# Modulation blocks computed two to a PSUM bank, and a new order for the opening stage of a two-layer trunk kernel

## Chip, cores, metric

The kernel runs on one core of one Trainium2 chip. The metric is the device time of one execution in microseconds (us); the time before is the median of three executions.

## What is computed

Two layers of a trunk are applied to 128 context tokens and 256 latent tokens of width 1024. Each layer is: a modulated RMSNorm and a SwiGLU feed-forward of width 2816, a modulated RMSNorm and a mixer (attention, a gated convolution of 31 taps, a long convolution with learned filters), and a second feed-forward. The parts that matter here:

```python
def trunk_layer(x, cond, l, P, cache):
    mod = (jax.nn.silu(cond) @ P['w_mod'][l] + P['b_mod'][l])[:, None, :]
    sh1, sc1, g1, sh2, sc2, g2, sh3, sc3, g3 = jnp.split(mod, N_MOD, axis=-1)
    h = rmsnorm(x, P['g_ffn1'][l]) * (1 + sc1) + sh1
    x = x + 0.5 * g1 * swiglu(h, P['w1_gate'][l], P['w1_up'][l], P['w1_down'][l])
...
def hyena_filters(L, w1, b1, f1, w2, b2, f2, w3, log_decay):
...
    h = jnp.sin(f1.astype(F32) * (z @ w1.astype(F32) + b1.astype(F32)))
    h = jnp.sin(f2.astype(F32) * (h @ w2.astype(F32) + b2.astype(F32)))
    h = (h @ w3.astype(F32)).reshape(L, HYENA_ORDER, 2, HYENA_W)
    decay = jnp.exp(log_decay.astype(F32)).reshape(HYENA_ORDER, 2, HYENA_W)
    h = h * jnp.exp(-tn[:, None, None, None] * decay[None])
```

The first feed-forward cannot start before the shift `sh1` and scale `sc1` of layer 0 exist for the slice of channels it contracts over. The filters depend on weights alone, and their spectra are needed much later, by the mixers.

## The kernel before

**Layout.** Activations lie with channels on the 128 partitions and the 384 tokens along the free axis: `x` is eight tiles of 128x384. Weights come as a stream of 512 KB chunks, each eight blocks of 128x128 (`raw`, five buffers). ScalarE casts a chunk to `hi` (L249), VectorE makes the remainder `lo` (L250), and each block is multiplied by three matmuls (`mm3`, L263 to L265): hi by hi, hi by lo, lo by hi.

**Opening.** `startup` (L1058) walks a list of letters, `STARTUP`, and issues what each stands for. A scheduler then places the instructions into the engines' queues; each engine runs its own queue strictly in the order given. The letters are: `z`, `c`, `e`, `w`, `f` load constants and filter weights; `M` with a number is one modulation block; `X` with a number loads one tile of `x`, makes its modulated form (`hidden`, L387, tile `h`) and its square; `G` is one step of the first matrix product, four column blocks times one `h`, 12 matmuls; `F` is the next piece of the filter generator; `R` and `S` are the norm; `D` with a number is a row of dummy matmuls on a matrix of ones (`spin`, L1053), as many as the tuple `SPIN` says, besides 12 at the start.

**A modulation block** (`mod_start`, L287) makes shift and scale of one of the eight channel tiles for both conditions. Two chunks of `w_mod` (tile `raw`, from `wms`) are multiplied by the 32-column matrix `scond`, of which two columns hold the conditions and 30 are zero, into four 32-row strips of a PSUM bank of tag `at` (L293). ScalarE copies the bank (L297), TensorE transposes it in two matmuls (L300), VectorE adds the strips up and finishes the numbers (L304, L310, L313). Every 32-bit matmul shows as two records in the profile.

**The filter generator** (`filters`, L946) yields after each piece. Two sine stages come first (L949 and L954 on TensorE, seven VectorE operations each, L938 on ScalarE). `filter_time` (L964) then makes three time groups per layer: ScalarE takes exponentials of the decay (L975, L976, tile `P`), TensorE makes two products that share the array by row halves (L979, PSUM tag `sp`, two banks), VectorE multiplies them (L984) and forms sums and differences (L990, tiles `hy` and `H`). `filter_freq` (L1013) makes three spectra per layer: two from those filters (L674), one from the 31 convolution taps, whose matmuls have 16 rows (L1032). Each spectrum goes through one buffer `sw` and is written to memory by a GpSimd-issued transfer (`Hd`, L1040), so a spectrum's buffer is free only when the previous one is written.

The rest (feed-forward, mixer, both layers) follows. Modulation of all later places is done on VectorE (L324) beside the matrix products.

Of the kernel before, what the change touches and what calls it, by code (L numbers as in the profile page):

```python
# [11 lines left out]
F32 = mybir.dt.float32  # L12
# [5 lines left out]
D, DEPTH, NP, NS, PAST = 1024, 2, 128, 256, 128  # L18
T = NP + NS
TB = T + 2  # L20
KT = D // 128
# [18 lines left out]
START_TILES = ["a0", "x11", "g0", "v0"]  # L40
PROGRAM = ("v1 x10 a1 H g1 H H q1 k q0 C v A C q3 q2 C A A H A H C A A x21 A V A A x20 C V A H C V C A V A W W W "
           "V V V W W W W W W W W W W W W W").split()
STARTUP = ("z c F F M4 D1 e M0 D2 w X0 M1 F M7 G M2 F X1 X2 M5 G M3 F X3 F F X4 F G M6 G X5 F G G F X6 X7 f G R F F S "
           "G F").split()
SPIN = (12, 3, 6)
LATE = {5: "cond", 12: "cst"}
MOD0 = {(0, 0): 5, (0, 2): 5, (1, 0): 5, (1, 2): 4}
RSTD = (3, 6)
# [144 lines left out]
class Kernel:  # L193
# [90 lines left out]

    def mod_start(self, kb):  # L287
        nc = self.nc
        ps = self.psum("at")[:, 0:256]
        for half in range(2):  # L290
            raw = self.raw(self.d["wms"][kb, half])
            for j in range(4):
                nc.tensor.matmul(ps[32 * j:32 * j + 32, :], lhsT=self.scond[:, half * 4 + j, :],  # L293
                                 rhs=raw[:, j * 256:(j + 1) * 256], start=half == 0, stop=half == 1,
                                 tile_position=(0, 32 * j))
        row = self.t(256)
        nc.scalar.copy(out=row, in_=ps)  # L297
        tp = self.psum("at")[:, 0:256]
        for b in range(2):
            nc.tensor.transpose(tp[:, b * 128:(b + 1) * 128], row[:, b * 128:(b + 1) * 128], self.ident)  # L300
        v = tp.rearrange("p (b j i) -> p b i j", b=2, j=4, i=32)[:, :, 0:2, :]
        for kind in range(2):
            m = self.mods[0, 0, kind][:, 2 * kb:2 * kb + 2]
            nc.vector.tensor_reduce(out=m, in_=v[:, 1 - kind], axis=AX.X, op=ALU.add)  # L304
            self.mod_finish(0, 0, kind, 2 * kb, 2)

    def mod_finish(self, l, sub, kind, o, n):
        nc = self.nc
# [704 lines left out]
    def filter_freq(self, l, G):  # L1013
        nc = self.nc
        cw = self.S("cv", (96, 768))
        nc.sync.dma_start(out=cw, in_=self.d["cw"][l])
        taps = self.S("P", (96, 512))
        for ri, op in enumerate((ALU.add, ALU.subtract)):
            ready = nc.vector.tensor_tensor(out=taps[:, ri * 256:ri * 256 + 256], in0=cw[:, 0:256], in1=cw[:, 256:512],
                                            op=op)  # L1020
        for o in range(3):
            H = self.S("sw", (128, 3, 512))
            if o < 2:
                src = [[G[o, t][:, ri * 256:(ri + 1) * 256] for ri in range(2)] for t in range(3)]
                U = self.dft(src[2], 2), self.dft(src[1], 1)
            else:
                U = self.psum("sp"), self.psum("sp"), self.psum("at")
                for ri in range(2):
                    for u, t in zip(U, (2, 1, 0)):
                        rows = slice(32 * t, 32 * t + 16)  # L1030
                        with self.tc.high_priority(offset=PAIR * (2 * ri + 2 - t > 0)):
                            mm = nc.tensor.matmul(u[:, ri * 256:ri * 256 + 256],  # L1032
                                                  lhsT=cw[rows, 512 + 128 * ri:640 + 128 * ri],
                                                  rhs=taps[rows, ri * 256:ri * 256 + 256], start=True, stop=True,
                                                  tile_position=(32 * t, 0))
                        if ri == 0 and t == 2:
                            self.after(mm, ready)
            self.butterfly(U[0], U[1], H[:, 2, :], H[:, 1, :])
            nc.scalar.copy(out=H[:, 0, :], in_=self.dft(src[0], 0) if o < 2 else U[2])
            nc.gpsimd.dma_start(out=self.Hd[l, o], in_=H)  # L1040
            yield
# [16 lines left out]
    def startup(self, cols, tags):  # L1058
        nc, cp = self.nc, self.cp
# [1 line left out]
        self.filt, self.decay, self.hs, box = self.filters(), {}, [], []  # L1061
        accs = [self.psum(t) for t in tags]
        self.idle = accs[3][:, 388:512]
        self.spin(SPIN[0])
        step = 0
        for n in STARTUP:
            k = int(n[1:] or 0)
# [12 lines left out]
            elif n == "c":  # L1080
                self.loaded.add("early")
                nc.sync.dma_start(out=self.csts[:, 128:EARLY], in_=self.d["cst"][:, 128:EARLY])
            elif n[0] == "D":
                self.spin(SPIN[k])
            elif n[0] == "M":
                self.mod_start(k)
            elif n[0] == "X":
# [16 lines left out]
    def run(self):  # L1104
        nc, cp = self.nc, self.cp
# [7 lines left out]
        nc.gpsimd.memset(self.ones, 1.0)  # L1113
        self.mhalf = cp.tile([128, 16], F32, name="mhalf")
        nc.gpsimd.memset(self.mhalf, -0.5)
        self.scond = cp.tile([128, KT, 32], F32, name="scond")
        nc.gpsimd.memset(self.scond, 0.0)
        nc.scalar.activation(out=self.scond[:, :, 0:2], in_=self.vec("cond", 0, 16).rearrange("p (k i) -> p k i", i=2),
                             func=AF.Silu)
        self.nsink = []  # L1120
        for l in range(DEPTH):
# [89 lines left out]
```

## Time and profile before

| | us |
|---|---|
| median of 3 executions | 1510.0 (1508.61 to 1513.52) |
| the profiled execution | 1510.81 |
| its span in the profile | 1509.0 |
| TensorE busy | 1482.5 (98% of the span) |
| VectorE busy | 1116.2 (74%) |
| ScalarE busy | 673.3 (45%) |
| first matmul of the first product step | at 27.52 |
| first matmul after the opening | at 72.70 |

Busy time is what the profile's records cover; a stretch in which TensorE reads as fully busy can still be slow when its granted clock is half. The granted clock is given as a share: 1.00 is 2.4 GHz, 0.50 is 1.2 GHz. "Idle before" in a row is how long the engine had stood still, with what ended the wait behind the arrow.

### The profile page before, as it was taken

To read this page: it belongs to the slowest core of one execution; us is meant where nothing else is said; L and a number is where in the kernel's file an instruction comes from. 1 tells how busy PE (TensorE), PEld (TensorE's weight loads), DVE (VectorE), ACT (ScalarE), POOL (GpSimd) and SP (SyncE) were. 2 spreads that over 40 slices of the span, in tenths; PEclk is the share of its full clock that TensorE was granted. 3 is DMA by queue.
4 is the path that set the end of the run, shared out by engine and by line. 5 is a ranking of instruction groups with operands and counts; after the bars stand their busy time and mean duration, and the time that the engine had idled before them with its cause. 6 is when DMAs were issued, how large, how long until landed. Compare 5 with 4: busy or idle time off the path is not lost.

```text
span 1509.0 us, 22131 instructions
## 1 busy us (share of the span) xinstructions
PE 1482.5 (98%) x8372; PEld 1401.0 (93%) x8372; DVE 1116.2 (74%) x2115; ACT 673.3 (45%) x1164; POOL 29.7 (2%) x72
## 2 busy tenths in 40 slices
PE   8999999999999999999999999999999999999997
PEld 4799999999968999999999999999996799999885
DVE  6799998776896789897558998755599577555342
ACT  6673333335476653224336333333547665333331
POOL 0100000000000000000000000000000000000000
PEclk9899999999999999999999999999999999999999
DMA  9847876565312357676444777644431135444531
GB/s 312 301 151 249 270 261 227 189 204 181 118 64 70 112 189 237 219 235 209 154 135 133 247 244 237 225 154 155 143 125 49 59 109 167 154 154 140 182 112 42
DMA packets 72651, 260.97 MB, mean 173 GB/s; under 512 B 8224, under 2 KB 9760, under 8 KB 72544
## 3 DMA queue, kind: packets, MB, share of 16 engines
q1 hardware_dynamic: 71360, 254.30, 51.4%
q0 software_dynamic: 1184, 5.25, 0.9%
q8 instruction: 66, 1.08, 0.3%
q14 instruction: 41, 0.34, 0.1%
HBM read 252.96 MB, written 6.56 MB: 172 GB/s over the span
## 4 chain that ended last, share of the span: by engine, by line
PE 92%; DVE 3%; ACT 3%; DMA 1%; issue 1%; SPq 0%; POOL 0%; POOLq 0%; DVEq 0%; ACTq 0%
PE acc L263 14%; PE acc L264 14%; PE acc L265 14%; PE S L265 12%; PE S L263 12%; PE S L264 12%; PE sp L474 2%; PE at L474 2%; PE sp L674 2%; PE acc L474 1%; PE S L474 1%; PE sp L720 1%; DVE lo L250 1%; DMA raw<-wmod 1%; DMA raw<-wms 0%
## 5 line engine op out<-in xcount | busy, mean ns | idle before, releaser
L250 DVE TENSOR_TENSOR lo<-raw,hi 128x1024 fp32r<-128x1024 f32 x313 | 381.7, 1222 | 209.1 <-ACT hi L249 160.2
L249 ACT CAST hi<-raw 128x1024 fp32r<-128x1024 f32 x313 | 327.0, 1049 | 390.7 <-issue 131.3
L324 DVE SCALAR_TENSOR_TENSOR junk<-raw,cb 128x1024 f32<-128x1024 f32 x256 | 312.7, 1221 | 49.8 <-DMA raw<-wmod 46.8
L263 PE MATMUL acc<-h,hi 128*128 128x384 f32 (+1 forms) x960 | 331.0, 345 | 0.0
L265 PE MATMUL acc<-h,lo 128*128 128x384 f32 (+1 forms) x960 | 326.0, 340 | 0.5 <-DVE lo L250 0.5
L264 PE MATMUL acc<-h,hi 128*128 128x384 f32 (+1 forms) x960 | 325.4, 340 | 0.6 <-DVE h L918 0.6
L263 PE MATMUL S<-h,hi 128*128 128x384 f32 (+1 forms) x768 | 259.9, 338 | 1.0 <-DVE x L435 1.0
L265 PE MATMUL S<-h,lo 128*128 128x384 f32 (+1 forms) x768 | 259.5, 338 | 0.0
L264 PE MATMUL S<-h,hi 128*128 128x384 f32 (+1 forms) x768 | 259.4, 338 | 0.0
L264 PEld LDWEIGHTS acc<-h,hi 128*128 128x128 f32 x960 | 181.0, 189 | 5.8 <-issue 3.1
L263 PEld LDWEIGHTS acc<-h,hi 128*128 128x128 f32 x960 | 180.5, 188 | 6.1 <-issue 3.9
L265 PEld LDWEIGHTS acc<-h,lo 128*128 128x128 f32 x960 | 181.5, 189 | 2.0 <-issue 0.8
L263 PEld LDWEIGHTS S<-h,hi 128*128 128x128 f32 x768 | 144.5, 188 | 2.0 <-issue 1.9
L265 PEld LDWEIGHTS S<-h,lo 128*128 128x128 f32 x768 | 145.0, 189 | 0.4 <-issue 0.3
L264 PEld LDWEIGHTS S<-h,hi 128*128 128x128 f32 x768 | 144.6, 188 | 0.4 <-issue 0.4
L393 ACT ACTIVATE h<-x,mod 128x128 fp32r<-128x128 f32 x96 | 41.5, 453 | 91.3 <-DVE x L435 89.4
L531 DVE TENSOR_TENSOR t<-S,t 128x384 f32<-128x384 f32 x72 | 39.8, 552 | 20.5 <-PE S L265 20.5
L281 ACT CAST P<-t 128x384 fp32r<-128x384 f32 x24 | 12.3, 514 | 71.4 <-DVE t L531 71.4
L530 ACT ACTIVATE t<-acc 128x384 f32<-128x384 f32 x72 | 34.8, 483 | 11.2 <-PE acc L265 11.2
L394 DVE SCALAR_TENSOR_TENSOR h<-x,mod,h 128x128 fp32r<-128x128 f32 x96 | 38.3, 415 | 1.2
L414 DVE TENSOR_TENSOR t<-acc,rb 128x384 f32<-128x384 f32 x44 | 24.3, 552 | 16.3 <-PE acc L265 16.3
L408 ACT ACTIVATE t<-t,mod,mod 128x128 f32<-128x128 f32 x64 | 31.7, 541 | 6.4 <-DVE t L405 6.4
(492 smaller groups left out, 2196.6 us busy)
## 6 DMA issues: line engine op xcount, KB each, us to landing
raw<-stream SPq DMA_DIRECT2D x313, 512.0 KB, 4.0
raw<-wmod SPq DMA_DIRECT2D x128, 512.0 KB, 4.3
raw<-wms SPq DMA_DIRECT2D x16, 512.0 KB, 6.6
Hd<-sw POOLq DMA_DIRECT2D x6, 768.0 KB, 4.6
H<-Hd SPq DMA_DIRECT2D x6, 768.0 KB, 4.9
x<-x SPq DMA_DIRECT2D x8, 192.0 KB, 6.2
y<-h SPq DMA_DIRECT2D x6, 256.0 KB, 2.1
cb<-crow SPq DMA_DIRECT2D x2, 512.0 KB, 5.3
```

Of the source, the lines that this page charges most:

```text
L249: nc.scalar.copy(out=hi, in_=raw)
L250: nc.vector.tensor_tensor(out=lo, in0=raw, in1=hi.bitcast(F32), op=ALU.subtract)
L263: nc.tensor.matmul(out, lhsT=w[0], rhs=x[0], start=start, stop=False)
L264: nc.tensor.matmul(out, lhsT=w[0], rhs=x[1], start=False, stop=False)
L265: nc.tensor.matmul(out, lhsT=w[1], rhs=x[0], start=False, stop=stop)
L324: nc.vector.scalar_tensor_tensor(out=self.junk, in0=raw, scalar=1.0, in1=self.cb[:, ci, :], op0=ALU.mult, op1=ALU.mult, accum_out=m[:, 2 * ...
L393: nc.scalar.mul(out=hl[:, 0, a:b], in_=self.x[k][:, a:b], mul=sc)
L394: nc.vector.scalar_tensor_tensor(out=hl[:, 1, a:b], in0=self.x[k][:, a:b], scalar=sc, in1=hl[:, 0, a:b].bitcast(F32), op0=ALU.mult, op1=AL ...
L408: nc.scalar.activation(out=t[:, a:b], in_=t[:, a:b], func=AF.Identity, scale=A[:, i:i + 1], bias=B[:, i:i + 1])
L474: nc.tensor.matmul(accs[b], lhsT=hid[2 * c + e][xi][:, b * 128:(b + 1) * 128], rhs=w[e][wi], start=c == 0 and left[b] == 5, stop=c == NFF ...
L530: nc.scalar.activation(out=s, in_=gp[:, :T], func=AF.Silu)
L531: nc.vector.tensor_tensor(out=s, in0=up[:, :T], in1=s, op=ALU.mult)
```

## The change

Three edits, all in the opening stage.

1. `mod_start` takes a pair of channel tiles. The matrix `scond` gets 34 columns, with the conditions in columns 2 and 3. The first tile of a pair multiplies by columns 2 to 33 and the second by columns 0 to 31, so their results fall on rows 0, 1 and rows 2, 3 of each strip and accumulate in one bank. One copy, one pair of transposes and one set of VectorE operations then serve two tiles. The 64 matmuls and the 16 chunks remain.
2. `STARTUP` is a new list: pairs in rising order, without the two rows of dummy matmuls, and with 10 dummies in place of 12 at the start.
3. The spectrum of the taps is made second of three instead of last.

```diff
-STARTUP = ("z c F F M4 D1 e M0 D2 w X0 M1 F M7 G M2 F X1 X2 M5 G M3 F X3 F F X4 F G M6 G X5 F G G F X6 X7 f G R F F S "
-           "G F").split()
-SPIN = (12, 3, 6)
+STARTUP = ("z c F F M0 e w X0 F X1 M1 F G F X2 G X3 F M2 F G X4 F G X5 M3 F X6 X7 G F G f F G R F F S G F").split()
+SPIN = 10
...
-    def mod_start(self, kb):
+    def mod_start(self, pair):
         nc = self.nc
         ps = self.psum("at")[:, 0:256]
-        for half in range(2):
-            raw = self.raw(self.d["wms"][kb, half])
-            for j in range(4):
-                nc.tensor.matmul(ps[32 * j:32 * j + 32, :], lhsT=self.scond[:, half * 4 + j, :],
-                                 rhs=raw[:, j * 256:(j + 1) * 256], start=half == 0, stop=half == 1,
-                                 tile_position=(0, 32 * j))
+        for e in range(2):
+            for half in range(2):
+                raw = self.raw(self.d["wms"][2 * pair + e, half])
+                for j in range(4):
+                    nc.tensor.matmul(ps[32 * j:32 * j + 32, :],
+                                     lhsT=self.scond[:, half * 4 + j, 2 - 2 * e:34 - 2 * e],
+                                     rhs=raw[:, j * 256:(j + 1) * 256], start=half + e == 0, stop=half + e == 2,
+                                     tile_position=(0, 32 * j))
...
-        v = tp.rearrange("p (b j i) -> p b i j", b=2, j=4, i=32)[:, :, 0:2, :]
+        v = tp.rearrange("p (b j i) -> p b i j", b=2, j=4, i=32)[:, :, 0:4, :]
         for kind in range(2):
-            m = self.mods[0, 0, kind][:, 2 * kb:2 * kb + 2]
+            m = self.mods[0, 0, kind][:, 4 * pair:4 * pair + 4]
             nc.vector.tensor_reduce(out=m, in_=v[:, 1 - kind], axis=AX.X, op=ALU.add)
-            self.mod_finish(0, 0, kind, 2 * kb, 2)
+            self.mod_finish(0, 0, kind, 4 * pair, 4)
...
-        for o in range(3):
+        for o in (0, 2, 1):
```

The lines of `mod_start` and above shift by one against the kernel before (L293 stays the line of the modulation matmuls; the copy is L298, the transposes L301, the exponentials L976 and L977, the half-array products L980, the tap matmuls L1033, the cast L248).

**ScalarE, from its first sine to the cast of the first weight chunk.** In the rows `cv` is the output of the second sine, `pt` the decay, `P` the exponentials, `sqs` and `t` after L343 and later squares of `x`, `h` the modulated `x`. Before:

```order
L938 ACTIVATE t_128<-t_131 128x384
L975 ACT_TABLE_LOAD
L975 ACTIVATE pt_181<-pt_181 128x512
L297 COPY t_168<-at_155 128x256
L976 ACTIVATE P_253<-pt_181,csts 128x512
L975 ACTIVATE pt_183<-pt_183 128x512
L938 ACT_TABLE_LOAD
L938 ACTIVATE cv_141<-t_144 64x384 x4
L297 COPY t_198<-at_185 128x256
L343 ACTIVATE sqs_226<-x 128x384
L976 ACT_TABLE_LOAD
L976 ACTIVATE P_254<-pt_183,csts 128x512
```

Now:

```order
L939 ACTIVATE t_126<-t_129 128x384
L939 ACTIVATE cv_139<-t_142 64x384 x4
L298 COPY t_178<-at_153 128x256
L976 ACT_TABLE_LOAD
L976 ACTIVATE pt_188<-pt_188 128x512
L344 ACTIVATE sqs_204<-x 128x384
L977 ACTIVATE P_208<-pt_188,csts 128x512
L394 ACTIVATE h_197<-x,mod_86 128x128
L394 ACTIVATE h_197<-x,mod_86 128x256
L976 ACTIVATE pt_190<-pt_190 128x512
L394 ACTIVATE h_224<-x,mod_86 128x128
L977 ACTIVATE P_209<-pt_190,csts 128x512
```

The two sines follow each other with no table load between them, and the two `pt` exponentials and the first `P` stand behind the second sine instead of ahead of it. Behind these rows, and still ahead of the cast of the first chunk (`hi_276`), now come the rest of `h_224`, one square, and the remaining four `P`.

**TensorE, up to the third half-array product.** `S` of L1055 is the dummy row, `at` a modulation bank, `sp` the products. Before:

```order
L293 MATMUL at_155<-raw_162,scond 32x256 x3
L300 MATMUL at_170<-csts,t_168 128x128 x2
L1055 MATMUL S_108<-ones 128x124 x3
L293 MATMUL at_185<-raw_186,scond 32x256 x4
L293 MATMUL at_185<-raw_192,scond 32x256 x4
L979 MATMUL sp_251<-kv_214,cv_141 128x512
L979 MATMUL sp_252<-kv_214,cv_141 128x512
L300 MATMUL at_200<-csts,t_198 128x128 x2
L1055 MATMUL S_108<-ones 128x124 x6
L293 MATMUL at_228<-raw_229,scond 32x256 x4
```

Now:

```order
L293 MATMUL at_153<-raw_172,scond 32x256 x4
L980 MATMUL sp_206<-kv_192,cv_139 128x512
L980 MATMUL sp_207<-kv_192,cv_139 128x512
L301 MATMUL at_180<-csts,t_178 128x128 x2
L293 MATMUL at_234<-raw_235,scond 32x256 x4
L293 MATMUL at_234<-raw_241,scond 32x256 x4
L980 MATMUL sp_292<-kv_192,cv_139 128x512
```

The dummies between the blocks are gone, and so is one pair of transposes.

**TensorE, at the tap matmuls of layer 0.** `acc` is the first product, `sqs` the sum of squares. Before:

```order
L362 MATMUL sp_664<-ones,sqs_226 128x1 x3
L1032 MATMUL sp_677<-P_557,cv_555 128x256 x2
L1032 MATMUL sp_678<-P_557,cv_555 128x256 x2
L263 MATMUL acc_105<-h_632,hi_648 128x386
L979 MATMUL sp_691<-kv_215,cv_141 128x512
L264 MATMUL acc_105<-h_632,hi_648 128x386
```

Now:

```order
L293 MATMUL at_462<-raw_481,scond 32x256 x4
L301 MATMUL at_489<-csts,t_487 128x128 x2
L1033 MATMUL at_563<-P_502,cv_500 128x256 x2
L1033 MATMUL sp_561<-P_502,cv_500 128x256
L1033 MATMUL sp_562<-P_502,cv_500 128x256
...
L980 MATMUL at_674<-kv_193,cv_139 128x512
L262 MATMUL acc_105<-h_414,hi_544 128x386
```

The cut leaves out the second matmul into each of `sp_561` and `sp_562`. All six tap matmuls now stand together, directly behind the last modulation pair and ahead of the fifth product step; before, two of them stood inside the fourth of the eight steps, and four ahead of the eighth.

## Rows read from the trace of the kernel before

**Rows 1.** The page: busy us, share of the span, instructions of each engine.

```profile
PE 1482.5 (98%) x8372; PEld 1401.0 (93%) x8372; DVE 1116.2 (74%) x2115; ACT 673.3 (45%) x1164; POOL 29.7 (2%) x72
```

**Rows 2.** Stretches of 10 us: busy us (instructions) per engine, granted clock, transfer share, GB/s.

```profile
10.00:20.00 10.00, 7.97 (x45) 3.57 (x46) 5.28 (x19) 8.46 (x14) 0.00 (x0) 0.83 1.03 399
20.00:30.00 10.00, 7.75 (x64) 4.33 (x63) 9.02 (x33) 9.37 (x17) 0.00 (x0) 1.00 0.84 285
...
60.00:70.00 10.00, 10.00 (x23) 5.09 (x19) 7.08 (x14) 5.14 (x9) 1.00 (x2) 0.56 0.71 252
```

**Rows 3.** What TensorE waited for, first 130 us: total us, times, longest.

```profile
PE at L293 <- DMA raw<-wms: 2.3, 2, 1.7
PE acc L265 <- DVE lo L250: 0.5, 1, 0.5
```

**Rows 4.** ScalarE in order of time: start us, us, line, operation, idle before.

```profile
11.05 1.28 ACT L975 ACT_TABLE_LOAD   x1
12.34 0.63 ACT L975 ACTIVATE pt<-pt 128x512 f32<-128x512 f32 x1
15.35 1.28 ACT L938 ACT_TABLE_LOAD   x1
16.64 2.15 ACT L938 ACTIVATE cv<-t 64x384 f32<-64x384 f32 x4
...
21.67 0.79 ACT L393 ACTIVATE h<-x,mod 128x128 fp32r<-128x128 f32 x2
...
24.89 1.32 ACT L976 ACTIVATE P<-pt,csts 128x512 f32<-128x512 f32 x2
26.12 0.35 ACT L297 COPY t<-at 128x256 f32<-128x256 f32 x1
26.37 1.04 ACT L249 CAST hi<-raw 128x1024 fp32r<-128x1024 f32 x1
...
31.95 0.94 ACT L346 ACTIVATE t<-x 128x384 f32<-128x384 f32 x2
```

**Rows 5.** VectorE in order of time, same columns.

```profile
15.69 0.36 DVE L936 TENSOR_SCALAR t<-t 128x384 f32<-128x384 f32 x1
...
27.86 1.22 DVE L250 TENSOR_TENSOR lo<-raw,hi 128x1024 fp32r<-128x1024 f32 x1
...
34.15 0.42 DVE L990 SCALAR_TENSOR_TENSOR hy<-P 128x256 f32<-128x256 f32 x1
```

**Rows 6.** TensorE in order of time, same columns.

```profile
14.24 0.44 PE L300 MATMUL at<-csts,t 128*128 128x128 f32 x2 [0.49 <-ACT t L297]
14.52 0.83 PE L1055 MATMUL S<-ones 128*128 128x124 f32 x6
15.28 1.07 PE L293 MATMUL at<-raw,scond 128*32 128x256 f32 x16
...
27.52 0.42 PE L263 MATMUL acc<-h,hi 128*128 128x386 f32 x1
...
59.16 1.45 PE L1032 MATMUL sp<-P,cv 16*128 16x256 f32 x8
...
63.56 0.53 PE L263 MATMUL S<-h,hi 128*128 128x386 f32 x1
63.88 0.53 PE L264 MATMUL S<-h,hi 128*128 128x386 f32 x1
...
72.70 0.44 PE L263 MATMUL acc<-h,hi 128*128 128x386 f32 x1
...
77.06 0.34 PE L263 MATMUL S<-h,hi 128*128 128x386 f32 x1
```

**Rows 7.** Stretches of 1 us on TensorE: busy us, granted clock, transfer share, GB/s.

```profile
61.00:62.00 1.00, 1.00 (x2) 0.60 0.71 172
...
71.00:72.00 1.00, 1.00 (x6) 0.78 0.91 324
```

**Rows 8.** The page's transfer issues: operation, count, KB each, us from issue to landing.

```profile
Hd<-sw POOLq DMA_DIRECT2D x6, 768.0 KB, 4.6
```

More of the change, by code (lines that the diff above doesn't have):

```diff
@@ L1063, in startup @@
         self.idle = accs[3][:, 388:512]
-        self.spin(SPIN[0])
+        self.spin(SPIN)
         step = 0
@@ L1082, in startup @@
                 nc.sync.dma_start(out=self.csts[:, 128:EARLY], in_=self.d["cst"][:, 128:EARLY])
-            elif n[0] == "D":
-                self.spin(SPIN[k])
             elif n[0] == "M":
@@ L1115, in run @@
         nc.gpsimd.memset(self.mhalf, -0.5)
-        self.scond = cp.tile([128, KT, 32], F32, name="scond")
+        self.scond = cp.tile([128, KT, 34], F32, name="scond")
         nc.gpsimd.memset(self.scond, 0.0)
-        nc.scalar.activation(out=self.scond[:, :, 0:2], in_=self.vec("cond", 0, 16).rearrange("p (k i) -> p k i", i=2),
+        nc.scalar.activation(out=self.scond[:, :, 2:4], in_=self.vec("cond", 0, 16).rearrange("p (k i) -> p k i", i=2),
                              func=AF.Silu)
```

## The prediction

> **What bounds the kernel now.** I read the page first: TensorE is busy for 1482.5 of 1509.0 us, VectorE for 74% [rows 1]. From 27.52 us on, TensorE reads as full almost to the end, so the sum of its work sets the end there, and a gain can come only from three things: an earlier start of that full stretch, less TensorE work in it, or a better clock. The new queues differ from the old only in the first 200 us or so; behind that they hold the same instructions in the same order. So I compare one mark: the first matmul behind the opening, at 72.70 us [rows 6]. What shifts it shifts the end.
>
> Second, the stretches of 10 us. Between 10 and 30 us TensorE is busy 7.8 to 8.0 us in ten, some of it with dummies, while ScalarE is busy 8.5 and 9.4 [rows 2]. The transfers run near full, yet TensorE waited for a modulation chunk only 2.3 us in all [rows 3]. So ScalarE's queue, not the arrival of bytes, sets when the first product step starts: its row that ends at 27.41 us is the cast of the first weight chunk, and the first product matmul follows at 27.52 [rows 4, 6].
>
> Third, the clock. Between 60 and 70 us the granted clock is 0.56 [rows 2]; it falls soon after 61 us and is back soon after 71 [rows 7]. The fall comes after the tap matmuls of 16 rows at 59.16. At 1.2 GHz product matmuls start 0.32 us apart (63.56 to 63.88); at 2.4 GHz, 24 of them take 77.06 - 72.70 = 4.36 us, 0.18 each [rows 6]. Ten us at half clock cost about 5.0 us.
>
> **The change, part by part.** The sum is made against the profiled execution, 1510.81 us with a span of 1509.0; it stands 0.8 above the median of 1510.0.
>
> 1. *Second sine.* Its table load ran from 15.35 to 16.63, and the last VectorE operation it depends on ended at 16.05 [rows 4, 5]. Without the reload, and with two fewer dummies ahead of the first sine (0.83/6 = 0.14 us for each record, four records, covered in part by the arrival of its input), the sine starts at about 15.85: **0.8 us earlier**. The rest of that load was waiting time anyway. The Trainium skill, "ScalarE: Activation LUTs", section "What ACT_TABLE_LOAD costs", puts a switch at about 2.66 us, a drain of 1.38 after the load included. The rows show the next activation 1.29 us after the load starts (11.05 to 12.34) and no drain, so the trace differs; by the page's figure the start of the product would come about 1.4 us earlier than I say.
>
> 2. *ScalarE from the second sine to the first cast.* The queue now holds behind the sine what was done in its shadow before: two `pt` exponentials (0.63 each) and one more `P` (0.66, half of 1.32). Two instructions for the second tile's `h` (0.7 of path, from 0.79) and one square (0.47, half of 0.94) also go ahead of the cast. One copy less returns 0.35 [rows 4]. That is 1.26 + 0.66 + 0.7 + 0.47 - 0.35 = **2.7 us later**. Together with step 1, the first product step starts at 27.52 - 0.8 + 2.7 = 29.4; I take 29.5.
>
> 3. *TensorE work from there to the mark.* It took 72.70 - 27.52 = 45.2 us. Off come 5.0 for the half clock, 0.5 for a wait on the first `lo` [rows 3], and 0.6 for the two pairs of transposes saved behind this point (at most 0.44 each [rows 6]). This leaves **39.1 us**. The modulation matmuls are as many as before, and at the first step half of them are done in both versions.
>
> 4. *Waits that the new order opens.* Behind the first two steps and the third pair's matmuls (29.5 + 24 x 0.18 + 2 x 1.07 = 36.0) stands the transform of the third time group. Its `hy` came 5.5 us after the end of the first `lo` (29.08 to 34.57 [rows 5]). `lo` now ends at about 30.7, and another tile's `h` (0.8) stands ahead, less 0.3 for small operations saved: ready at 36.7, a wait of 0.7. The last pair's transposes now stand directly behind its matmuls, so the copy is bare: 0.5, as at 14.24 [rows 6]. The fifth step's cast stands behind two squares and four `h` instructions that wait for those transposes: 0.94 + 1.6 + 1.04 of ScalarE and about 1.4 on VectorE, against 2.1 of tap matmuls and 0.9 of a lone half-array product; 0.8 is bare. A spectrum of the seventh step needs a bank that ScalarE empties only behind three casts and five exponentials: I put 1.1. Sum **3.1 us**; if VectorE and ScalarE run ahead it is 0, if each is half as long again 4.6.
>
> 5. *Dummies.* The nine in the middle filled holes (0.83 us for six records, at 14.52 [rows 6]); taking them out gains no time and leaves TensorE bare between about 14 and 28 us, with one hole of some 4.5 us: the second half-array products wait for VectorE to empty both `sp` banks, which waits for `P` exponentials that step 2 made late.
>
> 6. *Half clock.* The trace does not show the new order, so this is bounded. Below: none, since the two dense steps now follow the taps and TensorE stays warm in rows 2 from 20 to 30 with 7.75 us in ten. Above: the 5.0 of now, and 1 more in the first steps. I take **2.0**: TensorE probably falls in the hole of step 5, but is then waiting anyway, and probably once at the taps, but comes back sooner than before as dense steps follow.
>
> 7. *Queues.* The chunks keep their number, 16 of 512 KB; one 192 KB tile of `x` more goes ahead of the first weight chunk on SP (0.5 us at 399 GB/s [rows 2]), and the decay waits behind four modulation chunks in place of two. Both arrive before ScalarE asks. The write of each spectrum from GpSimd's queue moves with the spectrum; the third is wanted some 13 us behind the first, more than two writes of 4.6 take [rows 8]. Nothing on these queues is on the path; without that cover, 0.5.
>
> Mark: 29.5 + 39.1 + 3.1 + 2.0 = **73.7**, 1.0 later than 72.70. The profiled execution would be 1511.8, and on the scale of the median **1511.0**.
>
> **The rivals.**
>
> *A, faster.* TensorE keeps 2.4 GHz through the taps and the waits of step 4 close. The opening then holds only work: with the second sine's product at full clock (it lay in the stretch of 0.83 [rows 2]) the first step starts at 28.7, and 28.7 + 39.1 = 67.8, 4.9 before the mark: 1505.1. For it speaks that the fall at 61 us is 5 us of pure loss; against it, the two ScalarE microseconds of step 2. Chance 0.20.
>
> *B, slower: the clock.* The dummies held the clock up, and without them the hole of step 5 puts the array at 1.2 GHz when the first product step starts. 24 matmuls then cost up to 24 x (0.32 - 0.18) = 3.4, of which 0.7 falls into the wait of step 4; and the taps, with a lone half-array product and two waits around them, bring a second fall as long as the present one, 5.0. 29.5 + 39.1 + 2.4 + 2.7 + 5.0 = 78.7: 6.0 later, 1516.0. It decides against me once the half clock costs more than 6 us. The Trainium skill, "TensorE: Matmul & The Clock Gate", section "The HAM clock gate (the 'warmup' mystery)", states that the throttled clock is the default, which activity lifts and idleness brings back; rows 7 agree that the clock falls in a thin stretch, though there TensorE was not idle. Chance 0.22.
>
> *C, the edit does nothing:* the bytes of the opening, 285 to 399 GB/s [rows 2], set its end, and they are the same. Against it: TensorE's 2.3 us of waiting. 1510.0. Chance 0.13.
>
> **How the numbers follow.** My forecast has 0.45. About 0.3%, 4.5 us, is what a measurement of this kernel can tell from no change. Of the forecast 0.42 lies within that, 0.02 below and 0.01 above; with C, 0.55 is the same, with A 0.22 is faster, with B 0.23 slower. Range: the low end takes half clock and waits at 0 and a start at 28.7, which is rival A less 0.6 for the scatter of the median, 1504.5; the high end takes B and 1.5 for the waits at their bound of 4.6, 1517.5.
>
> **What would show it.** Right: one table load fewer on each side of the second sine; the sine at about 15.9; the first cast ending near 29.4 and the first product matmul right behind; a hole on TensorE before the second half-array products; the mark near 73.7. Wrong: a first product step before 28 us (step 2 fails), a clock of 1.00 from 30 us to the mark (step 6), or waits on chunks in place of ScalarE (C). If the mark lies before 69 us A holds, behind 77 B.

## The result and the profile after

The changed kernel takes **1521.33 us** (median of 7 runs, 1517.9 to 1527.61) beside 1512.82 for the kernel before in the same comparison (median of 7, 1508.61 to 1514.35). The ratio is **1.0067, interval 1.0053 to 1.0081**: slower by 0.67%, some 10 us. The forecast was 1511.0, within 1504.5 to 1517.5. The median lies outside, on the side of rival B. The forecast was made on a median of 1510.0 for the kernel before; as a ratio to that it was 1.0007, with an upper end of 1.0050, which is still below the interval measured.

The profiled execution took 1526.07 us. The first lines of its page, span and busy times, answer to [rows 1]:

```profile
span 1524.0 us, 22038 instructions
...
PE 1487.0 (98%) x8342; PEld 1404.1 (92%) x8342; DVE 1115.1 (73%) x2095; ACT 668.3 (44%) x1158; POOL 28.6 (2%) x72
```

Thirty matmul records fewer than in [rows 1], and yet 4.5 us more busy TensorE time: busy time grows when the clock falls. This one execution is slow for its kernel. Where the kernel before had a clock of 1.00 from 1160 to 1170 us, this one had 0.54, far behind the part that the change touches (the same work, some 12 us earlier before, had 1.00 there too). So the difference of the two spans, 15.0, is not the effect; I read the trace only up to 360 us and take sizes from the ratios.

ScalarE in order of time (start us, us, engine, line, operation; in brackets the idle time before it and who ended it), against [rows 4]:

```profile
9.50 0.52 ACT L939 ACTIVATE t<-t 128x384 f32<-128x384 f32 x1 [4.70 <-DVE t L937]
14.84 2.15 ACT L939 ACTIVATE cv<-t 64x384 f32<-64x384 f32 x4 [4.82 <-DVE t L937]
...
17.40 1.28 ACT L976 ACT_TABLE_LOAD   x1
...
27.72 1.05 ACT L248 CAST hi<-raw 128x1024 fp32r<-128x1024 f32 x1
```

The second sine starts at 14.84 in place of 16.64, with no table load in front of it; behind it the exponentials queue up, and the first cast ends at 28.77 in place of 27.41. Now TensorE, same columns, against [rows 6]:

```profile
23.44 2.08 PE L980 MATMUL sp<-kv,cv 64*128 64x512 f32 x4 [2.77 <-DVE P L985]
...
27.31 2.06 PE L980 MATMUL sp<-kv,cv 64*128 64x512 f32 x4
...
29.50 0.42 PE L262 MATMUL acc<-h,hi 128*128 128x386 f32 x1
...
47.98 0.48 PE L1033 MATMUL at<-P,cv 16*128 16x256 f32 x1
47.99 0.48 PE L1033 MATMUL sp<-P,cv 16*128 16x256 f32 x2
...
51.71 0.45 PE L262 MATMUL acc<-h,hi 128*128 128x386 f32 x1 [1.53 <-ACT hi L248]
...
56.80 2.07 PE L980 MATMUL at<-kv,cv 64*128 64x512 f32 x2 [3.24 <-ACT sw L1040]
...
77.13 0.41 PE L262 MATMUL acc<-h,hi 128*128 128x386 f32 x1 [0.96 <-DVE small L421]
```

The hole before the second half-array products is there (2.77). The first product step starts at 29.50, 0.73 after the cast that it needs: until then TensorE still had half-array products and transposes ahead of it, at 1.2 GHz (2.06 us for four records that took 1.13 in the kernel before). The mark, the first matmul behind the opening, comes at **77.13 in place of 72.70**. Between them stand the taps at 47.98, then a wait of 1.53 for a cast and one of 3.24 for a copy into `sw`. Before that copy, ScalarE itself had waited, and GpSimd's issues of the spectrum writes show for what:

```profile
55.67 0.58 ACT L681 COPY sw<-sp 128x512 f32<-128x512 f32 x1 [3.48 <-DMA Hd<-sw]
56.16 0.59 ACT L1040 COPY sw<-at 128x512 f32<-128x512 f32 x1
```

```profile
47.44 0.74 POOL L1041 DMA_DIRECT2D Hd<-sw  x1 [3.42 <-ACT sw L1040]
58.27 0.55 POOL L1041 DMA_DIRECT2D Hd<-sw  x1 [10.09 <-DVE sw L683]
68.33 0.53 POOL L1041 DMA_DIRECT2D Hd<-sw  x1 [9.52 <-ACT sw L1040]
```

The first spectrum's write was issued at 47.44 and its buffer was free at 55.67, 8.2 us later, against 4.6 from issue to landing in [rows 8]. The 4.6 is a median over the whole program. The first of these writes took as long, 8.4 us, in the kernel before, as its trace shows; there it held up ScalarE by 1.91 us, and TensorE shows no wait behind it:

```profile
41.52 0.72 POOL L1040 DMA_DIRECT2D Hd<-sw  x1 [40.29 <-DVE h L397]
```

```profile
49.91 0.58 ACT L680 COPY sw<-sp 128x512 f32<-128x512 f32 x1 [1.91 <-DMA Hd<-sw]
```

Last, stretches with their granted clock (the columns of [rows 2]):

```profile
20.00:24.00 4.00, 1.23 (x10) 0.51 (x4) 3.62 (x9) 4.00 (x10) 0.00 (x0) 0.50 1.04 414
24.00:28.00 4.00, 4.00 (x22) 1.10 (x20) 3.83 (x11) 3.32 (x7) 0.00 (x0) 0.50 0.50 162
...
52.00:56.00 4.00, 1.56 (x9) 1.24 (x8) 0.92 (x1) 0.52 (x2) 0.00 (x0) 1.00 0.95 368
56.00:58.00 2.00, 1.20 (x2) 0.50 (x2) 1.38 (x2) 2.00 (x4) 0.00 (x0) 0.63 0.16 64
58.00:60.00 2.00, 2.00 (x6) 1.20 (x5) 1.43 (x2) 2.00 (x4) 0.55 (x1) 0.50 0.35 146
60.00:62.00 2.00, 2.00 (x8) 2.00 (x7) 1.67 (x2) 2.00 (x4) 0.00 (x0) 0.50 1.00 325
62.00:64.00 2.00, 2.00 (x9) 1.97 (x8) 1.18 (x2) 0.56 (x1) 0.00 (x0) 0.66 1.00 334
```

Two falls to 1.2 GHz: an early one, over before the product steps, and a second one behind the waits at 51 to 57 us. The second costs about 0.95 + 0.6 + 1.0 + 0.7 = 3.2 us (half-array product, 58.8 to 60, 60 to 62, a third of 62 to 64).

Behind the mark more is lost: the broadcast copy of the next norm (`rb`) comes at 359.61 before and 367.21 now, 7.6 later. Of the 3.2 since the mark, about 1.7 are a half clock from 107.7 to 111.1 us, and 1.3 a wait at 139.8 for an `sw` copy; ScalarE had waited 3.9 for a write some 12 us earlier (4.1 in the kernel before, where TensorE did not wait).

### The profile page after: what moved, and what is told of

It is laid out like the page before. It is cut to its first block, busy times and chain, and to the rows that moved or that the text cites. A ratio compares the mean times of both kernels' runs of the same rounds, so it can differ in the third digit from the quotient of the medians.

```text
span 1524.0 us, 22038 instructions
## 1 busy us (share of the span) xinstructions
PE 1487.0 (98%) x8342; PEld 1404.1 (92%) x8342; DVE 1115.1 (73%) x2095; ACT 668.3 (44%) x1158; POOL 28.6 (2%) x72
## 4 chain that ended last, share of the span: by engine, by line
PE 69%; DVE 12%; DMA 11%; issue 5%; ACT 2%; SPq 0%; POOL 0%; DVEq 0%; POOLq 0%; ACTq 0%
PE acc L262 10%; PE acc L263 10%; PE acc L264 10%; DMA raw<-wmod 10%; PE S L264 8%; PE S L262 8%; PE S L263 8%; DVE junk L325 5%; DVE lo L249 3%; PE sp L475 2%; PE at L475 2%; PE sp L675 1%; DMA Hd<-sw 1%; PE acc L475 1%; PE S L475 1%
## 5 line engine op out<-in xcount | busy, mean ns | idle before, releaser
L248 ACT CAST hi<-raw 128x1024 fp32r<-128x1024 f32 x313 | 326.8, 1048 | 398.2 <-issue 139.3
```

The costliest lines, as they stand in the source:

```text
L248: nc.scalar.copy(out=hi, in_=raw)
```

## The experiments

The theories: **W**, waits: the spectra go through one buffer `sw`, and the new order (taps second among it) makes TensorE wait for its writes. **S**, sequence: the new list itself (late exponentials, blocks in clumps) costs. **D**, dummies: their removal drops the clock. **P**, pairs: a pair's chunk matmuls, copy and transposes in one piece cost. All runs were made in five rounds each, beside the kernel before (medians 1511.3 to 1512.5). "Old list" is the `STARTUP` of before, "new list" that of the change. "T2" means the tap spectrum second, "raw" the tap spectrum in two raw buffers.

| run | kernel | median us | ratio to before (interval) | mark us |
|---|---|---|---|---|
| - | changed kernel | 1521.33 | 1.0067 (1.0053-1.0081) | 77.13 |
| 1 | changed, taps last | 1522.14 | 1.0068 (1.0053-1.0084) | 76.66 |
| 2 | old list, T2 | 1509.97 | 0.9984 (0.9973-0.9994) | 69.30 |
| 3 | new list, unpaired, T2 | 1516.84 | 1.0036 (1.0022-1.0050) | 76.20 |
| 4 | changed, other bank | 1518.38 | 1.0043 (1.0026-1.0061) | 75.64 |
| 5 | changed, dummies back | 1520.57 | 1.0067 (1.0051-1.0082) | 77.39 |
| 6 | run 2 without dummies | 1514.37 | 1.0020 (1.0006-1.0035) | 69.69 |
| 7 | run 2, blocks rising | 1512.96 | 1.0011 (1.0003-1.0020) | 71.14 |
| 8 | run 2, pairs | 1524.56 | 1.0082 (1.0063-1.0101) | 78.95 |
| 9 | changed, raw | 1517.66 | 1.0036 (1.0024-1.0049) | 76.33 |
| 10 | run 8, raw | 1514.32 | 1.0016 (1.0005-1.0028) | 76.51 |
| 11 | run 2, raw | 1510.09 | 0.9982 (0.9970-0.9993) | 69.19 |
| 12 | run 9, decay first | 1519.98 | 1.0045 (1.0029-1.0061) | 75.18 |
| 13 | run 3, raw | 1516.47 | 1.0016 (1.0005-1.0027) | 75.20 |
| 14 | before, raw, taps last | 1513.81 | 1.0006 (0.9995-1.0017) | 72.64 |
| 15 | run 9, dummies at the taps | 1514.92 | 1.0019 (1.0007-1.0031) | 73.66 |

### Runs 1 to 4: one part undone, or done alone

Run 1, the changed kernel with the old order of spectra:

```diff
-        for o in (0, 2, 1):
+        for o in range(3):
```

> The changed kernel with the spectra in their old order (taps last). Theory W (write): with the taps second, their third product keeps a bank of tag `at` until ScalarE may overwrite the one buffer `sw`, which waits for the write of the first spectrum; TensorE stands 3.2 us at the lone half-array product behind that bank, and the half clock that follows costs 3.3 more. Then most of it goes: 4 to 7 us less than the changed kernel, 1514 to 1517 us, with no wait of TensorE on the copy into `sw`. Theory S (start): the new list costs its time by the late first step and the missing dummies; then the order of the spectra moves less than 2 us, 1519 to 1523.

Measured 1522.14, ratio 1.0068. The order of the spectra gives nothing back in the changed kernel. The early hole is there as in the changed kernel (3.3 us for `P`, in place of 2.77), and in place of the 3.24 at 56.80 TensorE waits 2.85 us at 57.39 for an `sw` copy: in the old order it is the second filter spectrum that finds the buffer still being written (ScalarE waits 4.22 for it). So this run does not speak against the buffer; it says only that the order of the spectra is not the cause here.

Run 2, that order alone in the kernel before:

```diff
-        for o in range(3):
+        for o in (0, 2, 1):
```

> The kernel before with the taps second of three, and nothing else. Theory W: slower than before by 3 to 7 us if the half-array products are again drawn ahead of the copy into `sw`, 1516 to 1520; if the queue keeps both of them together at the end of the opening, only the late write is left, 0 to 2 us. Theory S: within 2 us of before.

Measured 1509.97, ratio 0.9984: **faster than before** by 2.5 us, the contrary of W in its first form. The mark comes at 69.30 in place of 72.70, and from 60 to 70 us the granted clock is 1.00 where [rows 2] have 0.56:

```profile
60.00:70.00 10.00, 9.14 (x41) 6.00 (x40) 7.78 (x18) 6.91 (x12) 1.48 (x2) 1.00 0.89 269
```

The taps stand among product steps there. (This profile has a short fall of its own, 0.50 from 44 to 46 us; run 11 below has none and takes the same time.)

Run 3, the new list with unpaired blocks (`mod_start` of before; each pair's letter replaced by two blocks):

```diff
-STARTUP = ("z c F F M0 e w X0 F X1 M1 F G F X2 G X3 F M2 F G X4 F G X5 M3 F X6 X7 G F G f ...
+STARTUP = ("z c F F M0 M1 e w X0 F X1 M2 M3 F G F X2 G X3 F M4 M5 F G X4 F G X5 M6 M7 F X6 X7 G F G f ...
```

> The changed kernel's list, its 10 dummies and its order of spectra, but one modulation block at a time as before: only the pairing is undone. Theory W and theory S both put the loss elsewhere: then the pairing is worth its four pairs of transposes and four copies, and this is 0 to 3 us slower than the changed kernel, 1521 to 1525. If it is the pairing that costs (a pair's results come later than those of its first tile would), this is 4 us or more faster, 1513 to 1517.

Measured 1516.84, ratio 1.0036. List and lack of dummies cost about half; the pairs in this list cost the other half.

Run 4, the changed kernel with the half-array products of the second layer kept out of the `at` banks:

```diff
-            tag = "at" if l and t == 1 else "sp"
+            tag = "sp"
```

> The changed kernel, but the half-array products of layer 1's second time group take banks of tag `sp` as all others do, not `at`. The taps stay second. Theory W: the wait behind the bank goes (3.2 us) and with it the fall of the clock (3.3): 4 to 7 us less than the changed kernel, 1514 to 1517. Theory S: 1519 to 1523.

Measured 1518.38, ratio 1.0043, between the two expectations. The wait of 3.24 is gone, so the tap spectrum's third product did hold the `at` bank until `sw` was free; but others open (2.6 us for a cast, 1.6 for an `sw` copy). Some 3 us come back by the median; the interval overlaps that of the changed kernel, and the profiled execution comes to `rb` at 368.14, no earlier than 367.21. So a gain is not shown.

### Runs 5 to 8: dummies, rising order, pairs

Run 5, the dummies back in the changed kernel:

```diff
-STARTUP = ("z c F F M0 e w X0 ...
-SPIN = 10
+STARTUP = ("z c F F M0 D1 e D2 w X0 ...
+SPIN = (12, 3, 6)
```

> The changed kernel with the two rows of dummy matmuls (3 and 6) and the 12 dummies at the start put back, all else as changed. If the dummies kept the clock up and their removal is the cost (rival B of the prediction), the half clock between 16 and 28 us shrinks, the mark (first matmul behind the opening, 77.1 us in the changed kernel) comes back by 3 us or more, and the time falls to 1516 or less. If the new list and the pairs are the cost (my theory now), the half clock goes away only where TensorE waits anyway, the first product step stays at 29.5 or later, and the time stays within 1519 to 1524.

Measured 1520.57, ratio 1.0067, as without them. The first product step comes 1.0 earlier (28.54), the mark does not (77.39). The scheduler also put one `pt` exponential, with two table loads, back ahead of the second sine, so this run undoes a little more than the dummies; D, that their removal is what costs, falls for the changed kernel.

Run 6, the same removal in the old list of run 2:

```diff
-STARTUP = ("z c F F M4 D1 e M0 D2 w ...
-SPIN = (12, 3, 6)
+STARTUP = ("z c F F M4 e M0 w ...
+SPIN = (10, 0, 0)
```

> The kernel before with the tap spectrum second (the run that took 1510.0 us, mark 69.3) and, in addition, without the two rows of dummies and with 10 at the start: the same removal as in the change, but in the old list. Dummies as the cause: the half clock reaches the first product steps, the mark moves to 73 or later and the time to 1514 or more. List and pairs as the cause: mark 69 to 70.5, time 1509 to 1511.5.

Measured 1514.37, ratio 1.0020 beside run 2's 0.9984: there they are worth something (the time is that of the first expectation, the mark that of the second). Its runs spread from 1509.5 to 1520.8; the profiled one was among the fastest (1510.5). Its first product step starts 2.3 later than in run 2 (29.68 against 27.34), its mark only 0.4 (69.69), so how the dummies help the old list stays open.

Run 7, the old list with the blocks renamed into rising order, unpaired:

```diff
-STARTUP = ("z c F F M4 D1 e M0 D2 w X0 M1 F M7 G M2 F X1 X2 M5 G M3 F X3 F F X4 F G M6 G X5 ...
+STARTUP = ("z c F F M0 D1 e M1 D2 w X0 M2 F M3 G M4 F X1 X2 M5 G M6 F X3 F F X4 F G M7 G X5 ...
```

> The kernel before with the tap spectrum second, and its eight modulation blocks renamed into rising order at the places where blocks stood; unpaired, dummies kept, all other letters where they were. If the rising order itself costs, by the order in which chunks and channel numbers come, the time is 1513 or more. If the cost lies in where the blocks and the other letters stand (two blocks at a place, decay behind them, second sine's shadow empty), it stays at 1509 to 1511.5 with the mark near 69.

Measured 1512.96, ratio 1.0011, which falls between the two expectations: 2.7 to 3 us worse than run 2, so in the old list the rising order has a price of its own. Every kernel with the new list, and run 8 below, has the rising order too.

Run 8, the old list and its dummies with pairs at four of the eight places:

```diff
+STARTUP = ("z c F F M0 D1 e D2 w X0 F M1 G F X1 X2 G M2 F X3 F F X4 F G M3 G X5 F G G F X6 X7 f ...
```

> The kernel before with the tap spectrum second and its dummies and its order of steps, but with the blocks made in pairs by the changed code, four pairs at four of the eight places. If pairing itself is the cost (16 chunk products in one piece, copy and transposes bare, wider numbers late), the mark is near 74 and the time 1513 to 1517. If the cost is in the list alone, 1509 to 1511.5; four copies and eight transposes saved would give at most 1 us back.

Measured 1524.56, ratio 1.0082, above both expectations. That is 1.0% against run 2, but the pairs also come in rising order; against run 7, which has that order without pairs, it is **0.7%**, as much as the whole change. How is seen on TensorE, on ScalarE, and in the stretches behind:

```profile
64.28 0.34 PE L264 MATMUL S<-h,lo 128*128 128x386 f32 x1
64.56 1.13 PE L980 MATMUL at<-kv,cv 64*128 64x512 f32 x4
69.38 2.07 PE L675 MATMUL sp<-H,csts 128*128 128x256 f32 x4 [3.69 <-ACT sw L681]
```

```profile
68.74 0.59 ACT L681 COPY sw<-sp 128x512 f32<-128x512 f32 x1 [3.21 <-DMA Hd<-sw]
```

```profile
64.00:68.00 4.00, 1.69 (x8) 0.60 (x6) 1.04 (x3) 1.11 (x2) 0.00 (x0) 1.00 0.97 343
68.00:72.00 4.00, 2.07 (x4) 1.17 (x4) 2.64 (x4) 1.10 (x2) 0.00 (x0) 0.55 0.67 250
72.00:76.00 4.00, 3.10 (x6) 1.01 (x6) 2.14 (x5) 0.07 (x1) 0.59 (x1) 0.50 0.94 283
```

The last product step ends at 64.6. Nothing dense is left for TensorE, and the third spectrum stands behind the second one's write: 3.69 us idle, and then small matmuls at half clock. So W comes back in another form: not the order of the spectra, but that the blocks stand early and in clumps, so that no product steps are left beside the writes.

### Runs 9 to 11 and 13, 14: the buffer taken out of the way

There is no room for a second `sw`. The tap spectrum of the first layer (the middle one; in run 14 the last) goes into two of the five raw buffers instead, with its write in two transfers; the scheduler moves a few instructions behind it as a consequence. The same edit in five kernels (run 9 on the changed one):

```diff
-            H = self.S("sw", (128, 3, 512))
+            if l == 0 and o == 2:
+                HA, HB = (self.sp.tile([128, CHUNK * 128], F32, tag="raw", ...) for _ in range(2))
+                rows3 = HB[:, 0:512], HA[:, 0:512], HA[:, 512:1024]
+            else:
+                H = self.S("sw", (128, 3, 512))
+                rows3 = [H[:, i, :] for i in range(3)]
```

Run 9:

> The changed kernel, with the middle spectrum (that of the taps) kept in two of the five raw buffers in place of the one sw buffer, so that neither it nor the third spectrum waits for the write ahead of it. Theory now: the pairs and the new list bring the products of the opening forward, and what ends last is the chain of spectra through the one sw buffer, whose writes take 7 us and more there. Then the waits on the sw copies (3.2 us at 56.8, ScalarE's 3.5 and 3.9 us on the write) go, the mark comes from 77.1 to 74 or earlier, and the time falls to 1513 to 1518. Rival, the list and ScalarE's queue: the waits only move to other releasers, and the time stays at 1519 or more.

Run 10, run 8 with this edit:

> The run with pairs in the old list, with the middle spectrum in two raw buffers. There the twelve-matmul steps were done at 64.3 us, and TensorE then waited 5.2 us for copies into sw, with 68 to 77 us at half clock. If the one sw buffer is what pairing runs into, both go: the mark falls from 79.0 to 73 or earlier, the time from 1524.6 to 1511 to 1516. If the cost of pairing lies in its own matmuls, copies and transposes, it stays at 1520 or more.

Run 11, run 2 with it:

> The fastest kernel so far (the old list, unpaired, with the tap spectrum second), with the middle spectrum in two raw buffers. It waited 0.9 us for an sw copy in the opening. By the theory of the sw buffer 0.5 to 1.5 us come back, 1508.5 to 1510. If two of five raw buffers less starve TensorE of chunks, 1511 or more.

Run 13, run 3 with it:

> The new list with unpaired blocks (1516.8 us) and, in addition, the middle spectrum in two raw buffers. ScalarE waited 4.9 us there for the write from sw. If the one sw buffer costs this kernel too, it gains 2 us or more, to 1512.5 to 1515. If the sw wait is what the pairs alone run into, by bringing the products forward, it stays at 1515.5 to 1518; pairing then costs, without the sw wait, the difference to the 1517.7 of the same list with pairs: at most 1.5 us.

Run 14, the kernel before with it:

> The kernel before, tap spectrum last as it was, with that spectrum in two raw buffers. It waited 1.9 us on ScalarE for a write from sw, and its taps were followed by 10 us at half clock. If the gain of the tap spectrum made second came from that wait, the same gain comes here: 1509 to 1510.5 (ratio 0.998 to 0.999). If it came from the clock, because the taps stand among dense steps, the half clock stays at 61 to 71 us and the time at 1511.5 to 1513.

Ratios without and with the buffer in the way:

| kernel | one sw | raw | difference |
|---|---|---|---|
| old list, pairs | 1.0082 | 1.0016 | -0.66% |
| changed kernel | 1.0067 | 1.0036 | -0.31% |
| new list, unpaired | 1.0036 | 1.0016 | -0.20% |
| old list, T2 | 0.9984 | 0.9982 | -0.02% |
| before (taps last) | 1 | 1.0006 | +0.06% |

The one buffer costs 10 us in the old list with pairs and **4 to 5 us in the changed kernel**. In the old list with T2 and in the kernel before it costs nothing that shows: there the write lies beside product steps. In the unpaired new list the intervals overlap, and the medians (1516.84 and 1516.47) hardly differ, so the 0.20% is not shown. Run 10 in the stretches of run 8:

```profile
64.00:68.00 4.00, 3.26 (x17) 3.15 (x18) 3.28 (x4) 3.08 (x4) 0.00 (x0) 1.00 0.62 188
68.00:72.00 4.00, 3.62 (x17) 2.19 (x16) 3.61 (x5) 1.54 (x2) 0.54 (x1) 1.00 0.83 264
72.00:76.00 4.00, 3.26 (x11) 1.17 (x9) 2.74 (x8) 2.47 (x4) 0.00 (x0) 1.00 1.00 354
```

Busy 10.1 us of twelve in place of 6.9, at a clock of 1.00. The marks move less than I expected (76.33 and 76.51, where 74 and 73 were expected): both profiles start later than those they are compared with (first product step at 30.87 for 29.50, and 29.24 for 28.24), and part of the gain comes behind the mark, where in run 9 no half clock and no wait over 1 us is left up to 360 us.

Run 14 speaks on the gain of T2: the buffer was not it (1.0006 against 0.9984). The kernel before with the buffer freed still falls to half clock after its late taps (59.65 to 61.1), some 10 us on, behind half-array products and waits of 0.61 and 1.65; run 11 does not. Run 14's stretches, then run 11's:

```profile
72.00:74.00 2.00, 1.59 (x6) 1.54 (x6) 2.00 (x8) 1.98 (x3) 0.00 (x0) 0.50 1.04 399
74.00:76.00 2.00, 2.00 (x8) 2.00 (x8) 2.00 (x5) 1.57 (x5) 0.00 (x0) 0.50 0.65 264
```

```profile
64.00:68.00 4.00, 4.00 (x15) 1.77 (x13) 3.56 (x7) 3.69 (x6) 0.60 (x1) 1.00 1.01 358
68.00:72.00 4.00, 3.48 (x22) 3.36 (x21) 3.96 (x13) 2.30 (x7) 0.00 (x0) 1.00 1.01 352
```

### Runs 12 and 15: the start, and the clock behind the taps

Run 12, run 9 with the decay loaded first:

```diff
-STARTUP = ("z c F F M0 e w X0 ...
+STARTUP = ("z c F F e M0 w X0 ...
```

> The changed kernel with the middle spectrum in two raw buffers (1517.7 us, first product step at 30.9) and, in addition, the decay loaded ahead of the first modulation pair, so that the exponentials run in ScalarE's 4.7 and 4.8 us of waiting around the two sines, for two table loads more. If the late exponentials (step 2 of the prediction) carry the rest of the loss, the first cast comes 2 to 3 us earlier, the first product step at 28 or before, and the time falls to 1512.5 to 1515.5. If the start is hidden behind something later (the chain of spectra, the half clock), the first step comes earlier and the time stays at 1516.5 to 1519.

Measured 1519.98, ratio 1.0045: no gain. The first product step starts 2.8 us earlier than in run 9 (1.4 earlier than in the changed kernel, whose first sine came at 9.50 and not at 10.95 as in run 9), but the mark only 1.15 (75.18 against 76.33). The early start runs into a longer half clock:

```profile
28.07 0.44 PE L262 MATMUL acc<-h,hi 128*128 128x386 f32 x1
```

```profile
48.00:52.00 4.00, 2.63 (x10) 1.47 (x7) 3.59 (x11) 3.71 (x9) 0.41 (x1) 0.73 1.03 398
52.00:56.00 4.00, 4.00 (x9) 2.06 (x9) 2.67 (x5) 4.00 (x8) 1.09 (x2) 0.50 0.92 291
56.00:60.00 4.00, 4.00 (x14) 4.00 (x14) 1.31 (x2) 1.54 (x2) 0.00 (x0) 0.50 0.86 283
```

Run 15, run 9 with 12 dummies at the taps. These carry the start flag into the fourth bank of the product while its sums are being formed, and the outputs of this run are not those of the computation (that the flag is the reason is not shown). All instructions of the computation are there, so the run tells of time alone.

```diff
-STARTUP = ( ... X6 X7 G F G ...
-SPIN = 10
+STARTUP = ( ... X6 X7 D1 G F G ...
+SPIN = (10, 12)
```

> The changed kernel with the middle spectrum in two raw buffers (1517.7 us), and 12 dummies asked for where its tap matmuls stand, ahead of the fifth product step; the order written for TensorE puts 3 of them ahead of the last pair's transposes, 9 among the tap matmuls, and the lone half-array products behind the fifth and sixth step. If the half clock from 54 to 61 us (some 3.5 us lost) is what remains of the cost, it shrinks or goes, and the time falls to 1513 to 1515.5, less 1.7 us of dummies where nothing hides them. If the clock falls all the same, or the steps behind wait for ScalarE's casts as they did, the time is 1516.5 or more.

Measured 1514.92, ratio 1.0019: 2.6 us back by the ratios, though it holds more work. The same four stretches, first run 9, then run 15:

```profile
48.00:52.00 4.00, 3.01 (x24) 1.22 (x16) 2.53 (x13) 3.09 (x8) 0.74 (x1) 1.00 1.05 318
52.00:56.00 4.00, 2.91 (x8) 1.47 (x8) 3.18 (x6) 4.00 (x8) 0.64 (x2) 0.80 1.00 349
56.00:60.00 4.00, 4.00 (x12) 3.69 (x12) 2.22 (x3) 3.67 (x6) 0.46 (x1) 0.50 0.83 316
60.00:64.00 4.00, 4.00 (x19) 3.79 (x19) 0.51 (x2) 1.12 (x2) 0.00 (x0) 0.84 0.63 207
```

```profile
48.00:52.00 4.00, 4.00 (x30) 3.30 (x30) 2.73 (x13) 1.86 (x6) 0.41 (x1) 1.00 1.02 375
52.00:56.00 4.00, 3.41 (x23) 2.90 (x20) 3.30 (x6) 4.00 (x8) 0.55 (x1) 1.00 1.00 336
56.00:60.00 4.00, 4.00 (x23) 3.27 (x21) 0.38 (x1) 4.00 (x7) 0.54 (x1) 1.00 0.81 303
60.00:64.00 4.00, 3.78 (x20) 2.84 (x17) 3.97 (x6) 3.97 (x4) 0.00 (x0) 1.00 0.66 213
```

With the thin stretch at 48 to 53 us filled, the clock stays at 1.00, and 23 matmul records fit where 12 did. The lone half-array products moved with it to one place behind the sixth step, so the run changes two things that make TensorE thin, not the dummies alone; the intervals of runs 9 and 15 overlap a little. The profiled executions point the same way: `rb` comes at 360.07 against 363.85, 1.2 of it from an earlier start (29.70 against 30.87). The Trainium skill, "TensorE: Matmul & The Clock Gate", section "The HAM clock gate (the 'warmup' mystery)", states that idleness brings the throttled clock back; run 9 is in line with it (2.1 us without TensorE work between 48 and 54, ahead of the fall).

## Why the prediction was wrong

Of the changed kernel's 0.67%, the buffer accounts for 0.31 (run 9) and the clock behind the taps for perhaps 0.17 more (run 15, overlapping). What is left, 0.19% or 3 us, is not separated: with the buffer freed, the unpaired new list stands at 1.0016, and pairs in the old list too. What all of these share is the rising order of the blocks, which alone cost 2.7 to 3 us in the old list (run 7, 1.0011). That it costs the same in the new list is likely but not shown: no run put the blocks of the new list in another order.

1. *Second sine.* Right in direction, and more than twice the forecast: no table load, 1.8 us earlier (0.8 forecast), of which 1.0 is an earlier first sine (9.50 against 10.51). The step priced the two dummies saved at 0.14 us a record; at the start of the kernel they ran at some 0.23 (24 records in 5.48 us before, 20 in 4.54 now).
2. *ScalarE to the first cast.* The start of the products, 29.5, was forecast and came at 29.50, in part by luck: the cast ended at 28.77, 0.6 before the forecast, and the products waited 0.73 behind TensorE's own work at half clock, which the step didn't have. And run 12 shows that this step was not worth a term of the mark: 2.8 us of start gave 1.15 there, and nothing in the time.
3. *Work to the mark.* 77.13 - 29.50 = 47.6; less waits of 6.28 and half clock of 3.2 it is 38.1, where 39.1 was forecast. About right.
4. *Waits.* The sum was mis-sized, 6.3 against 3.1, and of the parts only two came: the bare copy (0.55 for 0.5) and the fifth step's cast (1.53 for 0.8). The wait for the third group's transform and the one for the `sp` bank did not come. In their place stand **3.24 for a copy into `sw`** and 0.96 at the mark.
5. *Dummies.* Right: their removal costs nothing in the new list (run 5), and the hole is there, 2.77 us (some 4.5 forecast).
6. *Half clock.* 3.2 to the mark and 1.7 behind it, against 2.0. It did fall in the hole, as said, though not quite without cost: up to 0.7 at the first product step (step 2). But "comes back sooner as dense steps follow" failed: what followed the taps was a wait of 1.53, nine matmuls and one of 3.24.
7. *Queues.* **This is the step that failed.** "Nothing on these queues is on the path": the cover was counted from the first spectrum to the third and with the 4.6 us of [rows 8]. Between them stands the tap spectrum, which needs the same buffer at once; the write took 8.2 us beside the chunk loads, as the same write had in the kernel before (41.52 to 49.91); and while the tap spectrum waits it holds banks that the half-array products need, in an in-order queue. With the old order of spectra the second filter spectrum stands there in its place, and costs as much (run 1). The step put at nothing, or 0.5 without cover, what run 9 prices at 4 to 5 us. It named the resource and the rows, and did not ask how long that one write takes, nor who holds a bank while waiting for it.

No rival was right either. B came nearest in time and mark (1516.0, 78.7), and the mark lies on its side of the line drawn at 77. But the dummies put back give nothing (run 5), which speaks against its mechanism, a clock lost with them, and its half clock, 5.0 at the taps and more at the first step, was 3.2. A's idea that the fall behind the old taps is pure loss holds in part, in another kernel: T2 in the old list removes it, and 2.5 of the 5 us come back. C, that the edit does nothing, is out: the interval is clear of 1.

Shown: the buffer's price in pairs and in the changed kernel (runs 8 to 11), that order of spectra and dummies are not it (1, 5). Run 12 shows no gain from an earlier start. Supported, with overlapping intervals: the clock behind the taps (15). Open: the last 3 us, for which the rising order is a candidate (7), and why the old list needs its dummies (6).

**The best version** is run 2, the kernel before with the one line of the spectra's order: 1509.97 us, 0.9984 (0.9973 to 0.9994), and again 0.9982 with the buffer freed (run 11). Both intervals exclude 1, but the gain is below the 0.3% that I called measurable.

## What to carry to other kernels

When work is moved forward, ask what it had been covering: in the old list the pairs cost little by themselves (run 10 with the buffer freed, 1.0016, beside the 1.0011 of run 7), but they used up the product steps that lay beside the writes of a single buffer. For each buffer that a queue empties, take the transfer's time from the row of that stretch and not from a median over the program, and follow one cycle to its end (issue, transfer under the load of that stretch, next writer, the bank that writer holds, the engine behind that bank) before calling a queue off the path. And put thin work (few rows, half arrays) between dense steps rather than after them: one line that did this in the old list was the only part of the change that paid.

## Unexpected on the chip

- Matmuls of 16 rows in different row groups ran beside each other when they stood together. In run 9 the taps run from 49.36 to 50.5, their records side by side; in run 15, at the same clock, the scheduler split them into two places, and they took 1.12 and 1.13 us. Run 9 and then run 15:

```profile
49.36 0.48 PE L1039 MATMUL at<-P,cv 16*128 16x256 f32 x1
49.37 0.48 PE L1039 MATMUL sp<-P,cv 16*128 16x256 f32 x2
```

```profile
48.20 1.12 PE L1039 MATMUL at<-P,cv 16*128 16x256 f32 x4
...
51.52 1.13 PE L1039 MATMUL sp<-P,cv 16*128 16x256 f32 x8
```

- The parts of the change don't add up: against run 2, pairs in rising order cost 1.0%, the new list without pairs 0.5%, both 0.8%. Each edit moves the waits of the other.
- The clock makes a single profile a poor measure of some us: in the changed kernel's profiled execution the half clock at 1160 to 1170 us alone lay where no instruction order differs from before.
